# Odd batches of an RWKV-7 layer get work tiles of their own, and projections and early stages alternate

## The chip, the cores and the metric

The kernel runs on one core of one Trainium2 chip. The metric is the device time of one execution in microseconds (us), median of three runs. The engines are TensorE (PE; PEld is its weight load), VectorE (DVE), ScalarE (ACT), GpSimd (POOL) and SyncE (SP), which issues nearly all DMAs. Each engine and each DMA queue works through its own list in order; between engines there are only semaphores.

## The reference

Two layers with 512 tokens and 1024 features, float32. Each layer is a mixer and a SwiGLU feed-forward block (2816 wide), each between two RMS norms and added to x. The mixer of layer 0 is RWKV-7, that of layer 1 a chunked spatial gating unit. The change lies in RWKV-7:

```
xs = x[None] + xx[None] * mix[:, None, None, :]           # six mixes of a token and the one before
r, k, v = einsum('cbtd,cde->cbte', xs[:3], w_rkv)
decay = exp(-exp(-softplus(-(w0 + tanh(xw @ w1) @ w2)) - 0.5))
a = sigmoid(a0 + (xa @ a1) @ a2);  g = sigmoid(xg @ g1) @ g2
kk = k * k_k / max(norm over a head, 1e-12);  k = k * (1 + (a - 1) * k_a)
S_t = S_{t-1} diag(decay_t) + (S_{t-1} (-kk_t)) (kk_t a_t)^T + v_t k_t^T;   y_t = S_t r_t    # per head, 64 x 64
y = group_norm(y) * gn_w + gn_b + sum(r * k * r_k) * v;   out = (y * g) @ w_o
```

## The kernel before

Products are made of three matmuls: each operand is split into a high part `whi` (ACT, a cast, line 131) and a low part `wlo` (DVE, line 132), and `mm3` (lines 156 to 158) adds high x high, high x low and low x high. Weights arrive as `wraw` (SP, line 138) into two buffers that take turns; the high and the low parts have two buffers each.

The recurrence is worked in chunks of 64 tokens. The 16 heads are cut into four batches of four heads (256 features), and a list of steps, PLAN, gives the order in which the code of the steps is written. A scheduler of the framework, which plays the written code against times of its own while it compiles, then sets the order of each engine's list; where it moves steps, only the lists show it. The steps of batch b:

- **P** (`kr_proj`): k and r of the batch, four groups of 24 matmuls named `proj` (features by tokens), each with one weight.
- **E** (`early`): the small products `w` and `a` (two of three matmuls each), tanh on ACT into `tw` and `ta`, a scan `cum` on DVE, exponentials `Pp` and `Pi`, the sum `ssp` of k squared (PE), Ln and Exp on ACT (a table load ahead of each), and the operands `ma`, `r`, `kk`, `kp` of the recurrence, which go to DRAM (`sa`, `sb`). `bps` is a small product for the bonus term.
- **X** (`mixed_split`): the mix for v, split into eight slices `xsp`, on ACT and DVE. **V** (`v_proj`): 96 matmuls `v` of a quarter of v's columns, with two weights; v goes to DRAM as `Vd`.
- **F** (`front`): loads the operands back (`ST`, `MV`, 64 loads of 64 KB in all) and makes the chunk matrices: `lm` and `bkt` on PE, copies to `LA`, `BX` and `MV`.
- **B** (`back`): inverts the triangular matrices. DVE transposes LA to `LX` and runs 15 steps of two small operations on `Dm`; transposes to `Dn` and `Dt`; then chained 32 x 32 products `Qp`, `Np`, `Tp`, `Q2p`, `T2p` with copies to `bdT`, and `mp` and `gh`, which give the final MV.
- **S** (`scan`): eight serial steps `us` and `Yp`. **N** (`finish`): group norm (`mu`, `va`, `nr_..`, `Y`), bonus (`vt`, `ob`) and gate (`yt`, `gate`).

The written order before is

```
P0 E0 P1 P2 E1 P3 E2 E3 X0 F0 B0 F1 V0 V1 V2 V3 B1 S0 F2 S1 F3 N0 B2 N1 B3 S2 N2 S3 N3
```

Tiles share rooms by tag: a tile with a tag waits until the oldest holder of the tag's buffers is free. `tw` and `ta` of every batch share two buffers `f0`, which Dm of F takes too; `cum` and `kp` share two buffers `gain` with MVt of B; the norm's scratch and Dn take two buffers `hn`; bdT has a room to itself and is cleared once, at the start. So two early stages cannot overlap: the second one's tw waits until the first one's ma is stored.

Of the kernel before, what the change touches and what calls it, by code (L numbers as in the profile page):

```python
# [7 lines left out]
F32 = mybir.dt.float32  # L8
# [5 lines left out]
P = 128  # L14
T = 512
# [4 lines left out]
C = 64  # L20
# [9 lines left out]
BANKS = dict(pa=(3, 4, 0, 7), pb=(1, 2, 5, 6), h0=(1, 2, 5, 6), h1=(3, 4, 0, 7), tr=(1, 2, 5, 6))  # L30
SLOTS = 17
E2 = 7
PLAN = "P0 E0 P1 P2 E1 P3 E2 E3 X0 F0 B0 F1 V0 V1 V2 V3 B1 S0 F2 S1 F3 N0 B2 N1 B3 S2 N2 S3 N3".split()
XV = "xxxessss"
XSLOTS = 13
LAG = 2
# [46 lines left out]
class Trunk:  # L83
# [287 lines left out]
    def rwkv(self, x0, nxt):  # L371
        nc, i, tc = self.nc, self.i, self.tc
        v, a, g = nc.vector, nc.scalar, nc.gpsimd
        mm = nc.tensor.matmul
        with ExitStack() as ctx:
            ep = ctx.enter_context
            rp = ep(tc.tile_pool(name="rp", bufs=1))
# [12 lines left out]
            def e2(name, shape=(P, 2, T), dt=F32):  # L390
                return rp.tile(list(shape), dt, name=name, tag="e2", bufs=E2)
# [7 lines left out]
            def gslot(name, shape):  # L399
                return self.gp.tile(shape, F32, name=name, tag="gain", bufs=2)  # L400
# [22 lines left out]
            g.memset(id32, 0.0)  # L423
            for r in range(0, P, 32):
                a.copy(id32[r:r + 32], self.ident[r:r + 32, r:r + 32])
            bdT = rp.tile([P, 16, 2, C], F32, name="bdT")
            g.memset(bdT, 0.0)


            w1 = s4("w1", [P, KT, 2, 64])  # L430
# [6 lines left out]
            for tt in range(TT):  # L437
                hn = e2("hn", (P, D))
# [149 lines left out]
            def small_split(name, src_fn, b):  # L588

                raw = rp.tile([P, 2 * P], F32, name=name, tag="ss_raw", bufs=1)  # L590
                src_fn(raw, slice(b * 2 * P, (b + 1) * 2 * P))
                hi = rp.tile([P, 2 * P], F32R, name=name + "h", tag="ss_hi", bufs=2)
                lo = rp.tile([P, 2 * P], F32R, name=name + "l", tag="ss_lo", bufs=2)
                self.split(hi, lo, raw)
                return hi, lo
# [12 lines left out]
            def early(b, k, r):  # L608

                wh, wl = small_split("wa2", load_wa2, b)  # L610
                pc = rp.tile([P, 2, NC], F32, name="pc", tag="pc", bufs=4)
                pr = lambda q: 2 * b + q
                fcs = lambda q: slice(q * P, (q + 1) * P)

                tw, ta = (self.f0p.tile([P, 2, T], F32, name=n, tag="f0", bufs=2) for n in ("tw", "ta"))
                for q in q2:
                    acc = self.bank("pe", "w")
                    self.mm3(acc, (wh[0:64, fcs(q)], wl[0:64, fcs(q)]), (hid[0:64, 0, :], hid[0:64, 1, :]), True, True)
                    a.activation(tw[:, q, :], acc, AF.Tanh, scale=0.5, bias=halfb[:, 0, pr(q):pr(q) + 1])
                for q in q2:  # L620
                    acc = self.bank("pe", "a")
                    self.mm3(acc, (wh[64:128, fcs(q)], wl[64:128, fcs(q)]), (hid[64:128, 0, :], hid[64:128, 1, :]), True, True)
                    a.activation(ta[:, q, :], acc, AF.Tanh, scale=-0.5, bias=halfb[:, 1, pr(q):pr(q) + 1])
                v.tensor_scalar(flat(tw), flat(tw), 1.0, None, op0=ALU.add)
                cum = gslot("cum", [P, 2, T])
                for q in q2:
                    v.tensor_tensor_scan(cum[:, q], rmask.rearrange("p c t -> p (c t)"), tw[:, q], 0.0, op0=ALU.mult, op1=ALU.add)
                Pp = e2("Pp", (P, 2, NC, C + 1))
                Ppf = Pp.rearrange("p q c t -> p (q c) t")
                g.memset(Ppf[:, :, 0:1], 1.0)  # L630
                a.activation(Ppf[:, :, 1:C + 1], flat(cum).rearrange("p (c t) -> p c t", t=C), AF.Exp, scale=-DECAY)
                Pi = cum
                a.activation(flat(Pi), flat(cum), AF.Exp, scale=DECAY, bias=lnh[:, 0:1])
                v.tensor_copy(pc, Pp[:, :, :, C])

                kp = gslot("kp", [P, 2, T])
                for q in q2:
                    v.tensor_scalar(kp[:, q, :], ta[:, q, :], hka[:, 0, pr(q):pr(q) + 1], hka[:, 1, pr(q):pr(q) + 1],
                                    op0=ALU.mult, op1=ALU.add)
                v.tensor_tensor(flat(kp), flat(kp), flat(k), op=ALU.mult)  # L640

                ri = tw
                for q in q2:
                    a.activation(ri[:, q, :], k[:, q, :], AF.Square, scale=fv("rwkv_k_k", pr(q)))
                    ssp = self.bank("pe", "ssp")
                    mm(ssp, bones, ri[:, q, :], start=True, stop=True)
                    v.tensor_scalar(ri[:, q, :], ssp, 1e-24, None, op0=ALU.max)
                a.activation(flat(ri), flat(ri), AF.Ln)
                a.activation(flat(ri), flat(ri), AF.Exp, scale=-0.5)
                kk = k  # L650
                for q in q2:
                    v.scalar_tensor_tensor(kk[:, q, :], k[:, q, :], nkk[:, pr(q):pr(q) + 1], ri[:, q, :], op0=ALU.mult, op1=ALU.mult)

                sv = lambda t: flat(t).rearrange("p (c t) -> p c t", t=C)
                ma = ri
                v.tensor_tensor(sv(ma), sv(kk), Ppf[:, :, 0:C], op=ALU.mult)
                v.scalar_tensor_tensor(flat(kk), flat(ta), -1.0, flat(kk), op0=ALU.add, op1=ALU.mult)
                v.tensor_tensor(flat(kk), flat(kk), flat(Pi), op=ALU.mult)
                bps = self.bank("pe", "bps")
                for q in q2:  # L660
                    v.scalar_tensor_tensor(ta[:, q, :], r[:, q, :], fv("rwkv_r_k", pr(q)), kp[:, q, :], op0=ALU.mult, op1=ALU.mult)
                    for c in range(NC):
                        tt, par = c // 2, c % 2
                        mm(bps[par * 64:par * 64 + 64, (tt * 2 + q) * 2:(tt * 2 + q) * 2 + 2], ta[:, q, c * C:(c + 1) * C],
                           hsel, start=True, stop=True)
                BN = rp.tile([P, TT, 2, 2], F32, name="bn", tag="bn", bufs=4)
                v.tensor_copy(BN.rearrange("p t q h -> p (t q h)"), bps[:, 0:16])
                v.tensor_tensor(sv(r), sv(r), Ppf[:, :, 1:C + 1], op=ALU.mult)
                v.tensor_tensor(flat(kp), flat(kp), flat(Pi), op=ALU.mult)
                nc.sync.dma_start(out=sa[b][0], in_=ma)  # L670
                nc.sync.dma_start(out=sa[b][1], in_=r)
                for hd in range(2):
                    for n, t in ((hd, kk), (1 - hd, kp)):
                        nc.sync.dma_start(out=sb[b][head[hd], :, :, n, :].rearrange("p q c t -> p (q c) t"), in_=sv(t)[head[hd]])
                return dict(pc=pc, BN=BN)

            def front(b, o):

# [50 lines left out]
            def back(b, o):  # L729

                MV, BX, LA, Dm = (o[n] for n in ("MV", "BX", "LA", "Dm"))
                LX = e2("LX", (P, 2, 528))

                v.transpose(full(LX), LA.rearrange("p q c (x t) -> p t (q c x)", x=2))
                LAu = LA.rearrange("p q c t -> p (q c) t")

                for r in (0, 64):
                    for z, x in ((r, 0), (r + 32, 32)):
                        a.activation(LAu[z:z + 32, :, x + 16:x + 32], LAu[z:z + 32, :, x + 16:x + 32], AF.Copy,
                                     scale=mk2[z:z + 32, 0, x + 16:x + 17])  # L740
                        g.memset(LAu[z:z + 32, :, x:x + 16], 0.0)
                LXd, Dmd = diag(LX), diag(Dm)
                for j in range(15):
                    n = 15 - j
# [201 lines left out]
            xr, kr, ops, Y = None, {}, {}, {}  # L946
            for n in PLAN:
                f, b = n[0], int(n[1])
                if f == "P":
                    if xr is None:  # L950
                        xr = mixed_split(0, "ssssssss")
                        xx.clear()
                    kr[b] = kr_proj(b)
                elif f == "E":
                    ops[b] = early(b, *kr[b])
                elif f == "X":
                    xs = mixed_split(2, XV)
                elif f == "V":
                    v_proj(xs, [b])
                elif f == "F":  # L960
                    front(b, ops[b])
                elif f == "B":
                    back(b, ops[b])
                elif f == "S":
                    if b == 3:
                        GW.append(gate_weights(b))
                        OB.extend(bonus(b, ops[b]))
                    Y[b] = scan(b, ops[b], (lambda y: finish_half(b, ops[b], y, (0, 1))) if b == 3 else None)
                elif b == 3:
                    finish_half(b, ops[b], Y[b], (2, 3))  # L970
                else:
                    finish(b, ops[b], Y[b])
# [166 lines left out]
```

## Time and profile before

| | |
|---|---|
| median of 3 runs | 1397.12 us (1393.59 to 1397.96) |
| profiled execution | 1395.72 us, its span 1394.0 us |
| mean granted TensorE clock | 0.971 of full speed |
| PE / PEld / DVE / ACT / POOL busy | 96% / 78% / 56% / 42% / 11% |
| RWKV layer, with its output projection | from the start to 487.67 us |
| projections P0 to P3 on PE | 48.78 to 156.68 us |
| scans: S0, S1, S2 begin | 263.3, 315.1, 379.5 us |

How the rows read. A row of grouped instructions has line, engine, operation, output <- input, shapes and count, then busy us and mean ns, and after the second bar the idle time of the engine just before them with the instruction that ended it. A row of the timeline has start, duration, engine, line and names; in brackets stands the idle time before it and what ended it; neighbours of one kind are merged, and a float32 matmul shows as two records. A row of windows has start and end, then length, busy time and number of records of PE, the granted TensorE clock, the busy share of the DMA engines and GB/s.

### The profile page before, as it was taken

The page shows a single profiled execution, that of the slowest core. Times are in us where ns is not written, and L with a number is a line of the kernel's source. Part 1 is how long each engine was busy: PE and PEld are TensorE (multiplying, and loading weights), DVE is VectorE, ACT ScalarE, POOL GpSimd, SP SyncE. Part 2 cuts the span into 40 slices and gives each one's busy share as a digit, 9 for nine tenths or more (in the row PEclk, how much of TensorE's full clock was granted, in tenths as well). Part 3 has the DMA queues.
Part 4 walks back from the last instruction along what each step waited for, and adds up shares of the span by engine and source line. Part 5 has one row for each costly group of instructions (what it writes and reads, how often), then busy time and mean ns, then how long its engine had stood idle before and what let it go on. Part 6 is the DMA issues. An engine that isn't in the chain of part 4 may idle for free.

```text
span 1394.0 us, 21544 instructions
## 1 busy us (share of the span) xinstructions
PE 1332.0 (96%) x8512; PEld 1088.7 (78%) x8512; DVE 783.9 (56%) x1373; ACT 579.2 (42%) x1076; POOL 152.6 (11%) x190
## 2 busy tenths in 40 slices
PE   5999979989799899999999999999999999999998
PEld 3677768878687688888888887878888888888886
DVE  7975776579847565544553225575574554453223
ACT  5665765566543453222322224543463332232121
POOL 5000200111000021111110002010121111110000
PEclk8999979989799999999999999999999999999999
DMA  5145375432214233333322332342223333332231
GB/s 150 36 140 148 108 208 166 127 77 69 92 49 158 61 101 112 91 95 102 91 91 91 103 109 76 107 138 89 91 77 93 103 91 93 103 92 91 91 105 61
DMA packets 209956, 142.00 MB, mean 102 GB/s; under 512 B 59536, under 2 KB 185024, under 8 KB 209856
## 3 DMA queue, kind: packets, MB, share of 16 engines
q1 hardware_dynamic: 208560, 135.91, 33.0%
q0 software_dynamic: 1296, 4.72, 1.0%
q8 instruction: 67, 1.10, 0.3%
q14 instruction: 33, 0.27, 0.1%
HBM read 124.35 MB, written 14.16 MB: 99 GB/s over the span
## 4 chain that ended last, share of the span: by engine, by line
PE 62%; DVE 2%; ACT 0%; issue 0%; DVEq 0%
PE gu L157 12%; PE gu L158 12%; PE gu L156 11%; PE acc L157 8%; PE acc L158 8%; PE acc L156 8%; PE u L158 1%; PE u L157 1%; PE u L156 1%; DVE x L273 1%; PE s L1065 1%; PE ptr L218 0%; DVE hT L59 0%; DVE rt L208 0%; DVE ry L209 0%; DVE hn L270 0%
## 5 line engine op out<-in xcount | busy, mean ns | idle before, releaser
L131 ACT CAST whi<-wraw 128x1024 fp32r<-128x1024 f32 x177 | 185.7, 1049 | 481.3 <-PE gu L157 250.5
L132 DVE TENSOR_TENSOR wlo<-wraw,whi 128x1024 fp32r<-128x1024 f32 x177 | 263.1, 1487 | 206.3 <-ACT whi L131 202.3
L156 PE MATMUL gu<-hT,whi 128*128 128x512 f32 (+1 forms) x768 | 288.8, 378 | 1.8 <-ACT hT L57 1.7
L157 PE MATMUL gu<-hT,whi 128*128 128x512 f32 (+1 forms) x768 | 288.5, 377 | 1.1 <-DVE hT L59 1.1
L158 PE MATMUL gu<-hT,wlo 128*128 128x512 f32 (+1 forms) x768 | 289.5, 378 | 0.0
L156 PEld LDWEIGHTS gu<-hT,whi 128*128 128x128 f32 x768 | 145.0, 190 | 31.5 <-ACT hT L57 2.3
L157 PEld LDWEIGHTS gu<-hT,whi 128*128 128x128 f32 x768 | 144.9, 189 | 30.5 <-DVE hT L59 1.5
L158 PEld LDWEIGHTS gu<-hT,wlo 128*128 128x128 f32 x768 | 145.1, 189 | 28.5 <-issue 0.2
L157 PE MATMUL acc<-wlo,act 128*128 128x512 f32 x416 | 164.0, 394 | 0.0
L156 PE MATMUL acc<-whi,act 128*128 128x512 f32 x416 | 163.5, 394 | 0.0
L158 PE MATMUL acc<-whi,act 128*128 128x512 f32 x416 | 160.4, 394 | 0.0
L332 DVE TENSOR_TENSOR sg<-sg,gu 128x512 f32<-128x512 f32 x44 | 30.3, 688 | 142.2 <-PE gu L158 139.2
L333 POOL TENSOR_TENSOR sg<-sg,hn 128x512 f32<-128x512 f32 x44 | 57.0, 1295 | 417.3 <-DVE sg L332 417.3
L156 PEld LDWEIGHTS acc<-whi,act 128*128 128x128 f32 x416 | 78.2, 188 | 18.1
L158 PEld LDWEIGHTS acc<-whi,act 128*128 128x128 f32 x416 | 78.2, 188 | 18.0
L157 PEld LDWEIGHTS acc<-wlo,act 128*128 128x128 f32 x416 | 78.1, 188 | 18.0
L330 DVE TENSOR_TENSOR sg<-gu,hn 128x512 f32<-128x512 f32 x44 | 30.4, 691 | 66.5 <-PE gu L158 66.3
L131 ACT CAST act<-sg 128x512 fp32r<-128x512 f32 x52 | 32.3, 621 | 71.7 <-POOL sg L333 57.5
L156 PE MATMUL proj<-xsp,whi 128*128 128x512 f32 x128 | 51.6, 403 | 0.0
L158 PE MATMUL proj<-xsp,wlo 128*128 128x512 f32 x128 | 51.1, 401 | 0.0
L157 PE MATMUL proj<-xsp,whi 128*128 128x512 f32 x128 | 50.3, 396 | 0.2 <-DVE xsp L132 0.2
L708 PE MATMUL lm<-MV,ST 128*128 128x128 f32 x256 | 40.0, 309 | 7.0 <-ACT BX L726 3.0
(303 smaller groups left out, 2124.0 us busy)
## 6 DMA issues: line engine op xcount, KB each, us to landing
wraw<-in_ffn_w_gate_dram SPq DMA_DIRECT2D x44, 512.0 KB
wraw<-in_ffn_w_up_dram SPq DMA_DIRECT2D x44, 512.0 KB, 3.8
wraw<-in_ffn_w_down_dram SPq DMA_DIRECT2D x44, 512.0 KB, 3.7
wraw<-in_rwkv_w_rkv_dram SPq DMA_DIRECT2D x24, 512.0 KB, 3.7
wraw<-in_sgu_w_in_dram SPq DMA_DIRECT2D x16, 512.0 KB, 3.7
x<-in_x_dram SPq DMA_DIRECT2D x8, 512.0 KB, 3.2
MV<-sa SPq DMA_DIRECT2D x64, 64.0 KB, 2.5
ST<-sb SPq DMA_DIRECT2D x8, 512.0 KB
```

The lines of the kernel that those rows point to most:

```text
L131: self.nc.scalar.copy(hi, src)
L132: self.nc.vector.tensor_tensor(lo, src, hi.bitcast(F32), op=ALU.subtract)
L156: mm(out, lhs[0], rhs[0], start=start, stop=False)
L157: mm(out, lhs[0], rhs[1], start=False, stop=False)
L158: mm(out, lhs[1], rhs[0], start=False, stop=stop)
L273: v.scalar_tensor_tensor(xts[tt][:, c], f, y[:, 0:1], xts[tt][:, c], op0=ALU.mult, op1=ALU.add)
L330: nc.vector.tensor_tensor(sg, pp[0], yb, op=ALU.mult)
L332: nc.vector.tensor_tensor(sg, sg, pp[1], op=ALU.mult)
L333: nc.gpsimd.tensor_tensor(sg, sg, yb, op=ALU.mult)
L708: mm(lm[:, cc * P:(cc + 1) * P], st[:, cc].rearrange("p n t -> p (n t)"), mv[:, :, cc, hd, :], start=True, stop=True)
L1065: mm(acc[:, tt * P:(tt + 1) * P], vt[tt][:, m * P:(m + 1) * P], wsT[:, m, :], start=True, stop=True)
```

## The change

Odd batches (E1, E3) get rooms of their own in the early stage: tw and ta are the two halves of a tile `tws` that lies in the room of bdT (new tag `bd`), and cum and kp lie in the two buffers `hn`. Even batches keep the old rooms. bdT is therefore taken and cleared when B0 begins, not at the start. And PLAN alternates: E1 is written ahead of P2, and E2 ahead of P3.

```diff
-PLAN = "P0 E0 P1 P2 E1 P3 E2 E3 X0 F0 B0 F1 V0 V1 V2 V3 B1 S0 F2 S1 F3 N0 B2 N1 B3 S2 N2 S3 N3".split()
+PLAN = "P0 E0 P1 E1 P2 E2 P3 E3 X0 F0 B0 F1 V0 V1 V2 V3 B1 S0 F2 S1 F3 N0 B2 N1 B3 S2 N2 S3 N3".split()
...
-            bdT = rp.tile([P, 16, 2, C], F32, name="bdT")
-            g.memset(bdT, 0.0)
+            bd = lambda name, shape: rp.tile(shape, F32, name=name, tag="bd", bufs=1)
...
-                tw, ta = (self.f0p.tile([P, 2, T], F32, name=n, tag="f0", bufs=2) for n in ("tw", "ta"))
+                if b % 2:
+                    tws = bd("tws", [P, 2, 2, T])
+                    tw, ta = tws[:, 0], tws[:, 1]
+                    room = lambda name: self.sm.tile([P, 2, T], F32, name=name, tag="hn", bufs=2)
+                else:
+                    tw, ta = (self.f0p.tile([P, 2, T], F32, name=n, tag="f0", bufs=2) for n in ("tw", "ta"))
+                    room = lambda name: gslot(name, [P, 2, T])
...
-                cum = gslot("cum", [P, 2, T])
+                cum = room("cum")
...
-                kp = gslot("kp", [P, 2, T])
+                kp = room("kp")
...
+            inv = []
...
+                if not inv:
+                    inv.append(bd("bdT", [P, 16, 2, C]))
+                    g.memset(inv[0], 0.0)
+                bdT = inv[0]
```

The number and kind of PE, ACT and DVE instructions stay the same; the scheduler's lists differ from P2 on. Three places, each as a list before and one of the change.

SP, the DMA queue, in the V stage. `wraw` of 128x4x256 is a V weight; sa and sb are stores of an early stage, MV, ST and BX loads of F. Before, ahead of the second V1 weight and the first V2 weight (the last row; the three V weights ahead of them came before any load of MV):

```order
L682 DMA ST<-sb 128x2x512
L674 DMA sb<-kp 1024x1x64 x2
L682 DMA ST<-sb 128x2x512
L689 DMA MV<-sa 64x4x64 x15
L702 DMA BX<-ident 64x4x64 x2
L583 DMA Vd<-vev 128x2x256
L670 DMA sa<-tw 128x1024
L583 DMA Vd<-vev 128x2x256
L138 DMA wraw<-in_rwkv_w_rkv_dram 128x4x256 x2
```

E3's store of ma is the row sa<-tw. In the change the last row is the pair of V2 weights (both V0 and both V1 weights came earlier); E3's stores of ma (sa<-tws), kk and r stand further up:

```order
L710 DMA BX<-ident 64x4x64
L680 DMA sb<-kp 1024x1x64 x2
L710 DMA BX<-ident 64x4x64 x7
L697 DMA MV<-sa 64x4x64 x13
L690 DMA ST<-sb 128x2x512 x2
L697 DMA MV<-sa 64x4x64 x3
L710 DMA BX<-ident 64x4x64 x2
L582 DMA Vd<-vev 128x2x256 x2
L138 DMA wraw<-in_rwkv_w_rkv_dram 128x4x256 x2
```

The V1 weights moved ahead of the loads, and V2's behind those of F0 and F1: from sa<-tws to the V2 pair there are 43 issues.

DVE, the end of B1's inverses, where N0's norm runs too. Before (Y less its mean, then the last copy to bdT, then the rest of the norm):

```order
L877 TENSOR_TENSOR Y<-Y,mu 128x1024
L716 TENSOR_TENSOR BX<-BX,mk_128 128x256
L805 COPY bdT<-T2p 32x16x32
L711 TENSOR_TENSOR MV<-lm,mk_128 64x4x2x64
L881 TENSOR_REDUCE va<-hn 128x16
L893 TENSOR_TENSOR hn<-hn,bn 128x4x128 x2
L165 TENSOR_SCALAR nr_a<-va 128x16
```

In the change:

```order
L173 SCALAR_TENSOR_TENSOR nr_t<-nr_t,nr_a 128x16
L174 SCALAR_TENSOR_TENSOR nr_y<-nr_t,nr_y 128x16
L895 TENSOR_TENSOR Y<-Y,nr_y 128x1024
L746 STREAM_TRANSPOSE LX<-LA 128x1024
L724 TENSOR_TENSOR BX<-BX,mk_128 128x256
L759 TENSOR_TENSOR tm<-LX,Dm 128x2x15
L761 TENSOR_TENSOR Dm<-Dm,tm 128x2x15
L817 COPY bdT<-T2p 32x16x32
```

The copy to bdT moved behind the whole norm and behind the transpose LX that begins B2.

DVE, the copies of B2's Tp and Q2p, where N1's norm and an output weight's split run too. Before:

```order
L881 TENSOR_REDUCE va<-hn 128x16
L749 TENSOR_TENSOR Dm<-Dm,tm 128x2x12x4
L893 TENSOR_TENSOR hn<-hn,bn 128x4x128
L165 TENSOR_SCALAR nr_a<-va 128x16
L893 TENSOR_TENSOR hn<-hn,bn 128x4x128
L747 TENSOR_TENSOR tm<-LX,Dm 128x2x55
L132 TENSOR_TENSOR wlo<-wraw,whi 128x1024
L167 TENSOR_SCALAR nr_h<-nr_a 128x16
L786 COPY bdT<-Tp 32x16x32
L749 TENSOR_TENSOR Dm<-Dm,tm 128x2x11x5
L169 TENSOR_SCALAR nr_y<-nr_h 128x16
L796 COPY Q_4024<-Q2p 32x512
```

In the change (LX and Dm belong to B3):

```order
L746 STREAM_TRANSPOSE LX<-LA 128x1024
L798 COPY bdT<-Tp 32x16x32
L724 TENSOR_TENSOR BX<-BX,mk_128 128x256
L887 TENSOR_REDUCE mu<-Y 128x16
L759 TENSOR_TENSOR tm<-LX,Dm 128x2x15
L132 TENSOR_TENSOR wlo<-wraw,whi 128x1024
L888 TENSOR_SCALAR mu<-mu 128x16
L761 TENSOR_TENSOR Dm<-Dm,tm 128x2x15
L889 TENSOR_TENSOR Y<-Y,mu 128x1024
L759 TENSOR_TENSOR tm<-LX,Dm 128x2x28
L808 COPY Q_4022<-Q2p 32x512
L798 COPY bdT<-Tp 32x16x32
```

Both copies of Tp and that of Q2p now stand ahead of va and hn, with one weight split between them.

## Prediction

> **What bounds the kernel now.** I read the page first, then a table of windows cut at stage borders, then the idle rows inside the two worst windows, then the DMA queue (SP) and VectorE (DVE) there. The page:
>
> ```profile
> span 1394.0 us, 21544 instructions
> PE 1332.0 (96%) x8512; PEld 1088.7 (78%) x8512; DVE 783.9 (56%) x1373; ACT 579.2 (42%) x1076; POOL 152.6 (11%) x190
> PE   5999979989799899999999999999999999999998
> ```
>
> TensorE (PE) is the bound: 96% busy, and from the fifteenth of the forty slices (34.85 us each) on it has no hole. What can be won lies in the first 488 us, the RWKV layer. Its stages (start and end; length, PE busy, granted clock, DMA share):
>
> ```profile
> 48.78:156.68 107.90, 107.73 (x493) 1.00 0.43 123
> 156.68:217.69 61.01, 52.05 (x366) 0.83 0.68 179
> 217.69:263.32 45.63, 42.67 (x732) 0.93 0.35 109
> 263.32:315.09 51.77, 46.05 (x797) 0.90 0.44 114
> 315.09:347.53 32.44, 30.83 (x395) 1.00 0.30 73
> 347.53:379.47 31.94, 24.03 (x425) 0.68 0.30 93
> ```
>
> The borders: first projection; first V matmul; first matmul of V's third column group (V2); first scan step of S0; of S1; end of S1's last step; first step of S2. The projections P0 to P3 run dense at full clock, so what E1 waits for today (rooms that E0 still holds) costs PE nothing. The losses are in the second row (9.0 us idle and clock 0.83: 52.05 x 0.17 = 8.8 us more, so 43.2 us of dense work take 61.0) and in the last (7.9 idle, clock 0.68). Who ends the idle time of the second:
>
> ```profile
> L157 PE MATMUL v<-wlo,xsp 128*128 128x256 f32 x64 | 21.1, 330 | 1.0 <-DVE wlo L132 1.0
> L708 PE MATMUL lm<-MV,ST 128*128 128x128 f32 x64 | 11.9, 354 | 5.5 <-ACT BX L726 3.0 <-POOL Dm L696 1.5 <-POOL Dm L695 0.7
> L664 PE MATMUL bps<-hsel,ta 128*64 128x2 f32 x64 | 2.8, 212 | 1.2 <-DVE ta L661 1.2
> L721 PE MATMUL bkt<-ident,ST 128*128 128x128 f32 x16 | 2.7, 291 | 1.0 <-ACT BX L715 1.0
> ```
>
> There E2 and E3 run their long DVE and ScalarE (ACT) chains between F0 and V. The change pulls E2 in front of P3, and gives E1 and E3 rooms of their own, so Dm of F0 no longer waits for E3's stores.
>
> **Term A, the V stage.** Ahead of V stand now E2's two ssp, its bps, and E3's twelve matmuls w and a, by these rows:
>
> ```profile
> 75.53 1.88 PE L646 MATMUL ssp<-tw,bones 128*128 128x512 f32 x4
> 136.31 1.10 PE L664 MATMUL bps<-hsel,ta 128*64 128x2 f32 x32
> 66.29 0.39 PE L158 MATMUL a<-hid,wa2l 64*128 64x512 f32 x1
> 66.53 0.39 PE L156 MATMUL a<-hid,wa2h 64*128 64x512 f32 x1
> 282.30 2.05 PE L708 MATMUL lm<-MV,ST 128*128 128x128 f32 x16
> ```
>
> 1.88 + 1.10 + 12 x 0.24 (start to start) = 5.9 us: V starts at 156.7 + 5.9 = 162.6. No wait is added in the projections: each weight is split one group of 24 matmuls ahead, and the first stage row has no idle time to lose. The order of the changed kernel puts two more units of F1's lm (2 x 2.05), four bkt and eight mvt (0.6 and 1.2 by the groups above) ahead of V2, 5.9 us that came after it before; that is as much as left. So dense work alone ends at 162.6 + 43.2 = 205.8 instead of 217.7. Two waits stand against it.
>
> First, X0's last two splits are written behind E3's k step (L652) on DVE, which waits for Ln and Exp on ACT:
>
> ```profile
> L652 DVE SCALAR_TENSOR_TENSOR k<-k,nkk,tw 128x512 f32<-128x512 f32 x4 | 2.8, 750 | 2.9 <-ACT tw L649 2.9
> 173.40 0.28 PE L664 MATMUL bps<-hsel,ta 128*64 128x2 f32 x4 [1.25 <-DVE ta L661]
> 176.00:180.00 4.00, 4.00 (x31) 0.50 0.83 214
> ```
>
> Bounds 0 (V gets there later) and 2.9 (it waits the step out); I take 2.7, since V reaches its seventh slice while that step runs. The other two rows show what a wait costs behind itself: after 1.25 us idle the clock is at 0.50. Six us at half clock are 3 us, added to each wait; 211.5. The Trainium skill ("TensorE: Matmul & The Clock Gate", Part 1) has the clock fall only after an idle window of about 3.4 us; by that these 3 us, and the next 3, would drop out and the sum would be 6 us better. The trace disagrees (1.25 us were enough), so I keep them.
>
> Second, V2's weights. SP issues in order:
>
> ```profile
> 184.55 1.88 PE L646 MATMUL ssp<-tw,bones 128*128 128x512 f32 x4
> 183.82 9.88 SPq L689 DMA_DIRECT2D MV<-sa  x15
> 196.95 0.33 SPq L670 DMA_DIRECT2D sa<-tw  x1
> 197.81 1.64 SPq L138 DMA_DIRECT2D wraw<-in_rwkv_w_rkv_dram  x2
> 205.69 2.34 DVE L132 TENSOR_TENSOR wlo<-wraw,whi 128x1024 fp32r<-128x1024 f32 x2
> ```
>
> One issue takes 9.88 / 15 = 0.66 us, and before, two V weights were stuck at 197.81 behind E3's store of ma. In the new order the V1 weights go ahead of F0's loads, but V2's come 43 issues behind E3's store. That store follows E3's ssp by 10.5 us (186.43 to 196.95): the ssp ends ten V matmuls and 1.88 us into V, about 165.7, so the store goes at 176 to 178; 43 x 0.66 = 28 us more, with a wait for E3's kp about 209. From issue to the first split's end took about 9 us at 197.81 (205.69 + 1.17); with DVE free perhaps 6.5: V2 starts at about 216 and not 211.5, and a second cold start costs 3. Bounds: 205.8 (weights in time) and 221 (9 us, and that split stands deep in the Dm loop). At 216 PE is 1.7 us early with 5.9 us more done, less 3: **A = -4.6 us**.
>
> The memset of bdT moves from the start into B0: 1.81 us on POOL, which is 11% busy, some 20 us ahead of the copy that needs it; without that cover it would cost its 1.8.
>
> ```profile
> 3.27 1.81 POOL L427 MEMSET bdT<- 128x2048 f32 x1
> ```
>
> **Term B, start of S1.** Before, B1's last bdT copy came ahead of most of N0's group norm on DVE; now the whole norm and the transpose LX of B2 stand ahead of it, and mp of B1 waits for that copy.
>
> ```profile
> 294.22 0.99 PE L778 MATMUL Np<-Qs,Dt 32*32 32x32 f32 x40
> 301.85 1.22 DVE L875 TENSOR_REDUCE mu<-Y 128x16 f32<-128x1024 f32 x1
> 307.55 0.69 DVE L805 COPY bdT<-T2p 32x512 f32<-32x512 f32 x1 [0.17 <-ACT bdT L805]
> 308.30 1.16 PE L810 MATMUL mp<-MVt,bdT 128*128 128x128 f32 x8
> 311.74 1.29 DVE L893 TENSOR_TENSOR hn<-hn,bn 128x512 f32<-128x512 f32 x2 [1.52 <-DMA hn<-Vd]
> 314.57 1.95 DVE L734 STREAM_TRANSPOSE LX<-LA 128x1024 f32<-128x1024 f32 x1
> ```
>
> S0 now ends ahead of Np, so mu can start near 293, not 301.85. From there: five large steps (four of 1.2, LX 1.95) 6.8; hn with its wait 2.8; four copies of 0.69, 2.8; eleven small ones at about 0.17, 1.9; two MV 1.4; ACT's square and copy 1.5: 17.2, with a later Vd load about 312. mp comes 3.7 late. Bounds 0 (B1 late anyway) and 8: **B = +4**, nearest to the count.
>
> **Term C, the gap between S1 and S2.** PE starves there for B2:
>
> ```profile
> 356.48 0.71 PE L781 MATMUL Tp<-Dt,Qs 32*32 32x32 f32 x36
> 359.87 0.69 DVE L893 TENSOR_TENSOR hn<-hn,bn 128x512 f32<-128x512 f32 x1 [1.67 <-DMA hn<-Vd]
> 361.34 1.22 DVE L132 TENSOR_TENSOR wlo<-wraw,whi 128x1024 fp32r<-128x1024 f32 x1
> 362.55 0.67 DVE L786 COPY bdT<-Tp 32x512 f32<-32x512 f32 x1
> 366.00 1.91 PE L801 MATMUL T2p<-bdT,Q 32*32 32x32 f32 x64 [0.29 <-ACT bdT L786]
> 379.47 0.33 PE L846 MATMUL us<-su,MV 128*64 128x64 f32 x2
> ```
>
> Tp ended at 357.2, its copies to bdT came at 362.55 behind hn (which waits for a load) and a weight split, and T2p at 366. In the new order these copies come ahead of va and hn, with Tp spread into S1's steps. T2p could run near 358, 8 us earlier; two splits of 1.22 still stand ahead of the last bdT copy, and N1's vt and yt ahead of S2 on PE. Bounds 0 and 10: **C = -5.3**. S3 and the rest are PE work in nearly the old order; I let them follow.
>
> **Sum:** -4.6 + 4 - 5.3 = -5.9 against the profiled execution's 1395.7: 1389.8. The median of the runs shown is 1.4 above that execution: **1391 us**.
>
> **Rivals.**
> 1. The V stage loses less, because both waits fall away: for it speaks that E2's chain is out of the stage and that the V1 weights now come early; against it the row of 15 issues. PE then reaches V2 at 205.8 instead of 216, 10 us and 3 of clock; B0's Dm loop on DVE, which cannot start before F0's last lm, takes about 5 back: 1383. On this the Trainium skill ("DMA: Bandwidth & Descriptors", Issuing engines are not separate DMA queues) says that a sequencer's time to start a DMA is usually small beside the DMA. The trace has 0.66 us for each of fifteen in a row. The clock rule cited above would give 1385 in the same place.
> 2. No change: A is won and B keeps it, with C at 0 because B2's mp still waits for N1's hn load: -4.6 + 4 + 0, with half a us of PE order either way: 1396 to 1398.
> 3. Slower: N0 on DVE becomes the bound of S1. If its Vd load lands 8 us later than I have it (it stands behind four loads of F3's MV on SP, which wait for S0's rooms), the last bdT copy, mp and S1 slip 12 us; F3 takes S1's rooms, so S2 and S3 slip too and C is lost: -4.6 + 12 = +7.4, 1404. It decides from a slip of about 9 us on. Against it: that load's wait was 1.52 before.
>
> **Chances.** What this kernel's timing can tell is about 0.3%, 4.2 us: faster is below 1392.9, slower above 1401.3. Forecast 0.45 (its own range 1386 to 1396, two thirds of it faster), rival 1 0.17, rival 2 0.20, rival 3 0.18. Faster 0.30 + 0.17 = 0.47; same 0.15 and 0.18 of rival 2, 0.33; slower the rest, 0.20. Range: half of rival 1, the forecast, rival 2 and the near part of rival 3: 1382 to 1402.
>
> **What the profile after would show.** A: V's first matmul near 162.6; idle of PE at a v matmul released by a DVE split near 173; the second pair of V weights issued near 209 and V2 starting near 216. B: LX ahead of the last bdT copy, mp of B1 near 312, S1 near 318. C: T2p of B2 within 10 us of S1's last step, the window from S1's end to S2 under 27 us, its clock above 0.68. I am wrong if V2 starts before 210 or after 221, if S1 starts before 312 or after 323, or if the gap before S2 stays at 32.

## The result and the profile after

The change makes the kernel slower: 1405.0 us against 1397.04 (medians of 11 runs each on the same chip; one run of before read 4482 us and is left out of the interval), ratio 1.0059, 95% interval 1.0042 to 1.0077, so 8 us. The forecast was 1391 and the range ended at 1402. The profiled execution took 1407.42 us, 2.4 above that median. Its page, in the rows shown of before:

```profile
span 1405.7 us, 21558 instructions
PE 1337.6 (95%) x8512; PEld 1092.1 (78%) x8512; DVE 785.2 (56%) x1373; ACT 577.2 (41%) x1076; POOL 152.7 (11%) x190
PE   5999988989789989999999999999999999999998
```

In the row of the forty slices (35.1 us each) little shows: the sixth, in the V stage, rose from 7 to 8, the seventh and the twelfth fell from 9 to 8 (and the fourteenth and the fifteenth changed places). The windows tell more; they are cut at the same events as before (but the first keeps before's 48.78, while the projections began here at 47.80, and the second ends where V2 runs on), and from S2 on three more (S2 to B3's first T2p; to the end of S3's steps; to the feed-forward block):

```profile
48.78:163.12 114.34, 113.39 (x538) 1.00 0.48 134
163.12:221.32 58.20, 47.82 (x363) 0.88 0.63 169
221.32:265.62 44.30, 42.52 (x718) 0.89 0.30 89
265.62:324.58 58.96, 50.20 (x789) 0.83 0.37 101
324.58:356.20 31.62, 31.06 (x540) 1.00 0.31 76
356.20:381.34 25.14, 17.72 (x240) 0.73 0.32 95
381.34:414.07 32.73, 29.70 (x589) 0.90 0.22 68
414.07:454.56 40.49, 38.13 (x375) 0.96 0.37 116
454.56:498.44 43.88, 38.91 (x174) 0.92 0.23 73
```

The same three stages of before:

```profile
379.47:405.72 26.25, 24.41 (x542) 1.00 0.19 59
405.72:441.95 36.23, 36.02 (x399) 1.00 0.40 126
441.95:487.67 45.72, 39.54 (x180) 0.96 0.24 76
```

S0's stage (fourth row) grew from 51.77 to 58.96 us and fell in clock from 0.90 to 0.83. The gap behind S1 (sixth) shrank from 31.94 to 25.14, as forecast. The three stages behind it grew by 6.5, 4.3 and -1.8. The feed-forward block starts 10.8 us later and takes 907.3 us instead of 906.3.

Since work moves between stages, lengths alone mislead. The next table has the time that PE lost in each stage, its length less busy time x clock, summed over the rows of a stage; "before held" and "after held" are the two kernels `rooms0` and `ctl` below, which run the lists of before and of after once more and show how far one profile can be trusted (FFN is the feed-forward block):

```
stage            before  before held  after  after held   mean, after less before
P0 to first V      0.2       0.5       1.0      0.9              +0.6
V to S0           24.2      22.5      23.0     20.3              -1.7
S0 to S1          10.3      10.0      17.3     18.9              +7.9
S1 and the gap    17.3      17.5      12.8     14.3              -3.8
S2 to FFN          9.6      11.6      18.6     14.8              +6.1
S0 starts        263.3     262.1     265.6    264.7              +2.5
S1 starts        315.1     313.6     324.6    324.6             +10.2
FFN starts       487.7     487.1     498.4    496.5             +10.1
```

All of the loss is there when S1 starts. Behind it the gain in the gap is taken back before the feed-forward block. A loss of PE's time names the stage in which it shows, not yet its cause.

### The profile page after: what moved, and what is told of

Same layout as the page of the kernel before. It is cut to its first block, busy times and chain, and to the rows that moved or that the text cites. A ratio compares the mean times of both kernels' runs of the same rounds, so it can differ in the third digit from the quotient of the medians.

```text
span 1405.7 us, 21558 instructions
## 1 busy us (share of the span) xinstructions
PE 1337.6 (95%) x8512; PEld 1092.1 (78%) x8512; DVE 785.2 (56%) x1373; ACT 577.2 (41%) x1076; POOL 152.7 (11%) x190
## 4 chain that ended last, share of the span: by engine, by line
PE 84%; DVE 7%; ACT 3%; DMA 3%; issue 2%; SPq 1%; POOL 0%; DVEq 0%; ACTq 0%; POOLq 0%
PE gu L158 11%; PE gu L156 11%; PE gu L157 11%; PE acc L156 9%; PE acc L157 9%; PE acc L158 9%; PE proj L158 2%; PE proj L156 2%; PE proj L157 2%; PE lm L716 2%; PE lora L506 1%; PE gh L829 1%; PE u L158 1%; PE u L156 1%; PE u L157 1%
## 5 line engine op out<-in xcount | busy, mean ns | idle before, releaser
L158 PEld LDWEIGHTS acc<-whi,act 128*128 128x128 f32 x416 | 78.2, 188 | 18.1
L157 PEld LDWEIGHTS acc<-wlo,act 128*128 128x128 f32 x416 | 78.1, 188 | 18.1
L156 PE MATMUL proj<-xsp,whi 128*128 128x512 f32 x128 | 51.8, 405 | 0.0
```

The lines of the kernel that those rows point to most:

```text
L156: mm(out, lhs[0], rhs[0], start=start, stop=False)
L157: mm(out, lhs[0], rhs[1], start=False, stop=False)
L158: mm(out, lhs[1], rhs[0], start=False, stop=stop)
```

## Experiments

After an ordinary edit the scheduler makes other lists, so that far more moves than was meant. So the experiments hold the lists: each kernel carries the order of every engine's list as a table, and ties each instruction to the one before it by an order alone, without a semaphore.

```diff
+    for e, text in LISTS.items():
+        own = [x for x in code if str(x.engine) == "EngineType." + engines[e]]
+        ...
+        row = [own[n] for n in np.cumsum(steps.astype(np.int64))]
+        for p, q in zip(row, row[1:]):
+            tc.add_manual_dep(q, p.name, how, reason="list")
```

Rooms and lists can so be taken apart, and single instructions moved. All ratios are to the kernel before on the same chip; kernels that ran on different chips are compared by these ratios.

### Rooms or lists, and from which stage on

`rooms0`: the rooms of the change (tws in `bd`, cum and kp in `hn`, bdT cleared in B0), all lists as before.

> The changed kernel's rooms and the written order of before, with every engine's list held exactly as in before (the one instruction left free is the clearing of bdT). It splits the change into its rooms and its lists. If the loss of 8 us comes from the lists alone: 1397 us, within 2 us of before. If the rooms themselves cost (a tile waits for its new holder, or bdT is cleared late): above 1400 us, with a new wait between 100 and 230 us.

Measured 1395.06 us, ratio 0.9998 (0.9983 to 1.0012). The rooms together with holding the lists cost less than 2 us by this interval; the loss comes with the lists. `ctl`, the lists of after held in the same way, is the partner of the later experiments:

> The changed kernel with every engine's list held exactly as it is: the comparison for the three runs beside it, since single executions of these kernels differ by up to 8 us. 1403 to 1407 us; a difference from the changed kernel's 1405 would be an effect of holding the lists.

Measured 1406.42, 1.0065 (1.0044 to 1.0087): like the change itself.

`ha_S0`, `ha_S1`, `ha_S2`: the lists of after up to the first step of S0, S1 or S2, and from there those of before. `hb_S1`: the lists of before up to S1, then those of after. Where two lists are joined there is a seam: what one has already done and the other not yet lands there.

> The changed kernel with its own lists up to the first step of S0 (265.6 us in its trace) and, from there, the lists of before on every engine, for what is then left. Theory 1 (the loss is made in three places, by lost TensorE time of each stage, after against before: +0.8 in the projections, -1.7 in the V stage, +0.5 up to S0, +7.0 in S0's stage, -1.0 in S1, -3.4 in the gap, +4.2 and +3.7 in S2 and S3): only -0.4 of it is kept here, so 1396 to 1399 us. Rival (the early lists set the later stages back whatever order follows): 1402 to 1406 us.

> The changed kernel's lists up to the first step of S1 (324.6 us), before's lists from there. Theory 1: S0's stage, with the copy to bdT behind N0's norm, costs 7.0 us; this run is 6 to 7 us above the run cut at S0, 1402 to 1405 us. Rival (what S0's stage loses is slack, since S1's gap to S2 waits for B2 anyway): within 2 us of the run cut at S0.

> The changed kernel's lists up to the first step of S2 (381.3 us), before's lists from there. Theory 1: the shorter gap gives 4.4 us back against the run cut at S1, so 1398 to 1401 us, and the lists of S2 and S3 are what costs the rest up to 1405. Rival (the gap was shortened only by leaving 6 us of TensorE work undone before S2, and S2 and S3 lose time because that work is still there): 1404 to 1406 us, no better than the changed kernel.

> The rooms of the change; the lists of before up to the first step of S1 (315.1 us in its trace), the changed kernel's lists from there. It is term C alone: B2's copies early on VectorE, the gap before S2 short. If the prediction's C holds: 1391 to 1393 us, faster than before by 4 to 5. Theory now, from the runs cut at S1 and of the whole change, which take the same time (1405): C gives nothing, since TensorE starts S2 earlier with as much less work done; 1395 to 1398 us, no difference from before.

```
kernel   median us  ratio (95%)               S0     S1     S2     FFN starts
ha_S0    1400.04    1.0030 (1.0015, 1.0045)   265.0  320.2  383.4  495.8
ha_S1    1404.95    1.0057 (1.0035, 1.0079)   265.2  324.9  384.3  496.1
ha_S2    1412.69    1.0108 (1.0089, 1.0128)   263.3  325.7  392.3  505.3
hb_S1    1412.43    1.0130 (1.0112, 1.0148)   260.4  324.5  382.9  497.9
```

With the new lists up to S1 alone the time is that of the whole change; up to S0 alone about half of the loss is there, which neither expectation had. From S1 to the feed-forward block ha_S1 took 171.2 us with the old lists and ctl 171.9 with the new: behind S1 the two are worth the same. The other two kernels are misses, since their seams cost more than what they were to show: in ha_S2 the left-over work of the gap stands ahead of S2, and in hb_S1 N0's vt, yt and gate and F3's lm stand ahead of S1, which starts 19.6 us behind B1's first mp instead of 6.8. They say nothing on the part of the gap. How much of ha_S0 and ha_S1 is their seam isn't known either: ha_S0 took 55.2 us from S0 to S1, with the old lists there, where before took 51.8.

### The V stage

In the changed kernel V1's matmuls end at 196.6, and V2 starts at 218.8. In order: PE's groups from there to V2; the queue SP (between its first row and the next stand 20 loads of F1); ACT and PE at the end of the stretch; and DVE:

```profile
L716 PE MATMUL lm<-MV,ST 128*128 128x128 f32 x48 | 9.1, 356 | 4.5 <-DMA ST<-sb 1.9 <-issue 1.6 <-ACT BX L723 1.0
L772 PE MATMUL mvt<-ident,MV 128*128 128x128 f32 x16 | 3.6, 388 | 2.7 <-ACT MVt L775 1.2 <-ACT BX L723 0.8 <-ACT BX L734 0.8
```

```profile
190.19 6.17 SPq L710 DMA_DIRECT2D BX<-ident  x7
...
209.90 1.08 SPq L582 DMA_DIRECT2D Vd<-vev  x2
211.28 1.25 SPq L138 DMA_DIRECT2D wraw<-in_rwkv_w_rkv_dram  x2
```

```profile
215.23 0.59 ACT L581 COPY vev<-v 128x512 f32<-128x512 f32 x1
217.01 0.58 ACT L581 COPY vev<-v 128x512 f32<-128x512 f32 x1
217.61 1.05 ACT L131 CAST whi<-wraw 128x1024 fp32r<-128x1024 f32 x1
```

```profile
218.83 0.78 PE L156 MATMUL v<-whi,xsp 128*128 128x256 f32 x2
221.32 0.58 PE L157 MATMUL v<-wlo,xsp 128*128 128x256 f32 x1 [1.72 <-DVE wlo L132]
```

```profile
211.77 0.69 DVE L719 TENSOR_TENSOR MV<-lm,mk 64x512 f32<-64x512 f32 x1 [4.27 <-PE lm L716]
```

V2's weights were issued at 211.28, 2.3 us later than forecast (209). V0's stores to Vd (L582) stood in the same row of issues, at 209.90. The room that V1's results are copied to (`vev`, two buffers) comes free with them, so V1, done at 196.6, left its banks only at 215.2 and 217.0, and the cast of V2's first weight stands right behind the second of these copies. Until then PE had F1's products alone, with waits (7.2 us in the two groups), and the last row shows DVE, in the middle of B0's Dm loop, waiting 4.27 us for one of them.

`v2fill` mends this in the new lists: on SP V0's stores and V2's weights go ahead of seven BX loads and F1's loads, on PE V2's matmuls fill the stretch, and two of F1's groups of products go behind B0's Qp; the copies and splits on ACT and DVE follow. Stores and weights move together, so it doesn't tell the one from the other.

```
 SP:  sb<-kp x2
+     Vd<-vev x2            (issued at 189.41)
+     wraw<-in_rwkv_w_rkv x2    (at 192.27)
      BX<-ident x7
      MV<-sa x13 ... ST<-sb x2 ... MV<-sa x3
      BX<-ident x2
-     Vd<-vev x2
-     wraw<-in_rwkv_w_rkv x2
```

> The changed kernel's lists with the V stage's end put in another order: on SP the stores of V0 and the loads of the V2 weights go ahead of seven BX and all F1 loads (before, 30 and 27 issues later); the casts, splits and evacuations of V1 to V3 follow on ScalarE and VectorE; on TensorE 64 matmuls of V2 fill the stretch from 198 to 215 us, in which F0's last unit and mvt wait; F1's first two units move behind Qp of B0 and Q2p, so that B0's 15 steps run without their copies between. Term A: if the store of V0 and the V2 weights, stuck on SP, are what the V stage lost, Qp of B0 comes near 219 to 222 (228.65), S0 near 257 to 260 (265.62), and the kernel takes 1397 to 1400 us. Rival (the stretch is bound by F1's operands and rooms, so what V2 fills is missing later): S0 within 2 us of 265.6 and 1403 to 1407 us.

Measured: B0's first Qp at 219.33 (226.41 in ctl, 228.65 in the change), S0 at 260.2 (264.7 in ctl), S1 319.3, S2 376.6, S3 416.4, FFN 493.5 (496.5). The median is 1404.31, ratio 1.0057 (1.0043 to 1.0072) beside ctl's 1.0065: about 1 us, which these intervals don't tell from nothing. S0 comes where the theory had it and the time where its rival had it: the stage can be shortened by 4.5 us in this way, but that gives back little of the loss.

### The start of S1

B1's last steps and N0 on DVE, in the changed kernel, and when PE waited for them:

```profile
298.04 1.22 DVE L887 TENSOR_REDUCE mu<-Y 128x16 f32<-128x1024 f32 x1 [1.01 <-ACT Y L873]
...
306.53 1.29 DVE L905 TENSOR_TENSOR hn<-hn,bn 128x512 f32<-128x512 f32 x2 [2.32 <-DMA hn<-Vd]
307.94 0.69 DVE L798 COPY bdT<-Tp 32x512 f32<-32x512 f32 x1
...
313.51 1.95 DVE L746 STREAM_TRANSPOSE LX<-LA 128x1024 f32<-128x1024 f32 x1
...
316.15 0.69 DVE L817 COPY bdT<-T2p 32x512 f32<-32x512 f32 x1
```

```profile
309.29 2.02 PE L813 MATMUL T2p<-bdT,Q 32*32 32x32 f32 x64 [0.90 <-ACT bdT L798]
...
316.89 1.16 PE L822 MATMUL mp<-MVt,bdT 128*128 128x128 f32 x8 [0.78 <-DVE bdT L817]
```

N0 starts with mu (first row). Not one copy of B1 but three stand behind parts of it: the second of Tp waits out the Vd load of hn (2.32 us), and T2p with it, 12.7 us behind Np instead of 10.8. From T2p to mp it is 7.6 us instead of 3.3, since the last copy waits for the norm and for LX ahead of it on DVE.

`b_before` tests the last copy by itself, in the lists of before, by moving one DVE instruction behind N0's hn products:

```diff
-L817 COPY bdT<-T2p
 L719 TENSOR_TENSOR MV<-lm,mk
 L893 TENSOR_REDUCE va<-hn
 L905 TENSOR_TENSOR hn<-hn,bn x2
 L165 TENSOR_SCALAR nr_a<-va
+L817 COPY bdT<-T2p
```

> The lists of before, held, with one instruction moved: on VectorE the last bdT copy of B1 goes behind N0's two hn products and nr_a (from 307.5 to about 313 us), which is term B by itself. If the chain from B1's mp over S1 and F3's loads to B3 and S3 sets the end: mp, S1 and S3 5 to 6 us later and the time 4 to 6 us above before, 1401 to 1403. Rival (B3 has slack: its transposes end 16.6 us ahead of its Qp in the trace of before): S1 later by as much, S3 and the time within 2 us of before.

Measured 1402.52, ratio 1.0038 (1.0023 to 1.0052), 5 us slower. The copy and PE's wait for it, first in rooms0, then in b_before:

```profile
306.09 0.69 DVE L817 COPY bdT<-T2p 32x512 f32<-32x512 f32 x1 [0.17 <-ACT bdT L817]
306.83 1.16 PE L822 MATMUL mp<-MVt,bdT 128*128 128x128 f32 x8
```

```profile
311.42 0.69 DVE L817 COPY bdT<-T2p 32x512 f32<-32x512 f32 x1
312.25 2.05 PE L822 MATMUL mp<-MVt,bdT 128*128 128x128 f32 x8 [5.72 <-DVE bdT L817]
```

A copy 5.3 us later makes mp 5.4 later, S1 7.4 later (321.06 against 313.62, though S0 had begun 1.3 earlier) and the program about 5, as expected. In the lists of before, what delays that copy delays the end.

The other direction, in the lists of after: `bcopy` moves B1's copies (bdT, Q) ahead of N0's norm on DVE, and the ACT partner of the last one; `fixAB` is bcopy and v2fill together.

```diff
 L165 TENSOR_SCALAR nr_a<-va
-L798 COPY bdT<-Tp
+L798 COPY bdT<-Tp x2
+L808 COPY Q<-Q2p
 L167 TENSOR_SCALAR nr_h<-nr_a
 ...
+L817 COPY bdT<-T2p
 ...
 L761 TENSOR_TENSOR Dm<-Dm,tm
-L817 COPY bdT<-T2p
```

> The changed kernel's lists with four copies to bdT and Q2 moved, and nothing else: on VectorE the second Tp copy, the Q2 copy and the last bdT copy of B1 go ahead of the rest of N0's norm and of B2's transpose, on ScalarE the other last bdT copy goes ahead of two LA copies. Term B: if the order of these copies costs what the prediction said, mp of B1 comes 4 us earlier (near 313 instead of 316.89), S1 near 320.5, and the kernel takes 1400 to 1402 us. Rival (S1 starts late because B1 as a whole is late, and N0's norm must be done then or soon after): S1 within 1.5 us of 324.6 and 1404 to 1406 us.

> Both edits of the two runs before this one. If A and B are separate and each as large as thought: the sum of the two gains against the changed kernel, 1392 to 1397 us, as fast as before or faster. If they overlap (the same wait counted twice): no better than the better of the two.

Measured 1406.28 (1.0082, 1.0059 to 1.0105) and 1405.10 (1.0071, 1.0047 to 1.0096): nothing gained beside ctl's 1.0065. In bcopy T2p came 3 us earlier and the copy 2.5 us behind it, but:

```profile
306.30 1.20 PE L813 MATMUL T2p<-bdT,Q 32*32 32x32 f32 x64
...
312.24 2.05 PE L716 MATMUL lm<-MV,ST 128*128 128x128 f32 x8 [2.75 <-ACT BX L723]
...
314.94 1.91 PE L822 MATMUL mp<-MVt,bdT 128*128 128x128 f32 x8
```

On PE lm and vt still stand ahead of mp, and lm waits for ACT's copies. S1 started at 324.69 (324.57 in ctl).

`s1fix` therefore puts the end of B1 (copies, mp, gh, and the first steps of S1) ahead of most of N0 and of half of F3's lm, on all engines; `v2s1` is s1fix and v2fill.

> The changed kernel's lists with B1's end put ahead of N0 on all engines: the bdT and Q2 copies as in the run before, and now also, on TensorE, mp and gh of B1 and the first steps of S1 ahead of N0's transposes vt and yt, its gate products and half of F3's lm; VectorE's additions to MV, ScalarE's copies of mp and the store of N0 on SP follow. Theory 2: mp comes near 312 (316.9), S1 near 318 (324.6), the second unit of F3's loads, which waits for B1's additions, near 318 (324.7), LX of B3 some 5 us earlier than 356.7, and the time is 4 to 7 us under the control run. Rival (N0 has to be done at that place in any case, for its rooms, and only changes places with S1): S3 within 2 us of the changed kernel's and the time as the control run's.

> The V stage's end reordered (V2 early) and B1's end ahead of N0, both on the changed kernel's lists. If theory 2 holds and the V stage's gain of 3 to 5 us at S0's start goes through the same chain: 8 to 11 us under the control run, 1394 to 1397 us, as fast as before. If the V stage's gain is lost in S0's stage as in the earlier run: as the run with B1's end alone.

Measured 1413.90 (1.0122, 1.0092 to 1.0153) and 1412.57 (1.0113, 1.0090 to 1.0136), both worse than either expectation. The copy came in time, mp at 313.2, S1 at 321.6, but S1 then ran for 43.8 us instead of 31.4:

```profile
321.56:365.36 43.80, 41.18 (x554) 0.81 0.22 54
```

What was put off now stands between S1's serial steps.

The last try was in the lists of before. `t2_first` puts B1's T2p on PE between the halves of one lm group, and its copies, mp and gh earlier on all engines:

```diff
-L716 MATMUL lm<-MV,ST x8
+L716 MATMUL lm<-MV,ST x4
 L813 MATMUL T2p<-bdT,Q
+L716 MATMUL lm<-MV,ST x4
+L822 MATMUL mp<-MVt,bdT x4
```

> The lists of before, held, with B1's end moved up: T2p goes between the two halves of the lm group that stands ahead of it on TensorE (305.0 to about 303.3 us), its two copies to bdT, the first mp, gh and the additions to MV follow. If B1's chain alone sets S1, F3's rooms and S3: mp 2 to 3 us earlier, S1 and S3 2 to 3 us earlier, 1393 to 1394 us, 0.15 to 0.25% under before. Rival (another chain, N0's products and F3's lm on TensorE ahead of S1, ends at the same time): mp earlier, S1 and the time within 1 us of before.

Measured 1399.45, 1.0027 (1.0011 to 1.0043). T2p came 40.0 us behind S0's first step instead of 41.7, and mp 43.7 instead of 45.0, but S1 53.2 instead of 51.8: N0's and F3's products on PE end no earlier. That is the rival, and the time is worse than the rival had it; in this execution T2p also took 1.92 us, 1.20 in rooms0, so part of it can be the clock. No version beat the kernel before.

### The gap behind S1

`slowc` undoes the third place in the lists of after: B2's copies of Tp and Q2p go behind N1's hn products again.

```diff
-L798 COPY bdT<-Tp
 ...
 L759 TENSOR_TENSOR tm<-LX,Dm
-L808 COPY Q<-Q2p
-L798 COPY bdT<-Tp
 ...
 L905 TENSOR_TENSOR hn<-hn,bn x2
+L798 COPY bdT<-Tp
+L808 COPY Q<-Q2p
+L798 COPY bdT<-Tp
```

> The changed kernel's lists with C undone by itself: on VectorE the two Tp copies and the Q2 copy of B2 go behind N1's two hn products, as they stood before, and on ScalarE their partners follow. T2p of B2 comes 4 to 6 us later and with it S2 (381.3 in the changed kernel's trace). Theory 2 (the end is set by the chain gh of B1, rooms of F3, F3's loads and lm, B3, S3, on which B2 and S2 do not lie): S3 and the time stay within 2 us of the control run. Rival (the prediction's sum: what S2 loses, the kernel loses): 4 to 6 us above the control run.

Measured 1411.06, 1.0098 (1.0074 to 1.0121), 4.6 us above ctl on the same chip, as its rival had it; the two intervals just overlap. B2's T2p, in ctl and in slowc:

```profile
368.05 1.92 PE L813 MATMUL T2p<-bdT,Q 32*32 32x32 f32 x64 [0.70 <-ACT bdT L798]
```

```profile
376.24 1.92 PE L813 MATMUL T2p<-bdT,Q 32*32 32x32 f32 x64 [0.43 <-ACT bdT L798]
```

S2 moved from 381.5 to 389.5, 7.9 us, of which S1 was 2.9 late already. So in the new lists that place is worth about 5, near its forecast 5.3.

`c_before` does it alone in the lists of before: the copies ahead of hn, and on PE B2's T2p ahead of N1's vt and mp ahead of its second vt and of yt.

```diff
+L798 COPY bdT<-Tp
+L808 COPY Q<-Q2p
+L798 COPY bdT<-Tp
 L905 TENSOR_TENSOR hn<-hn,bn
 L165 TENSOR_SCALAR nr_a<-va
 ...
-L798 COPY bdT<-Tp
-L808 COPY Q<-Q2p
-L798 COPY bdT<-Tp
```

> The lists of before, held, with C alone: B2's Tp and Q2 copies on VectorE ahead of N1's hn products and of a weight's split, their partners on ScalarE and the last bdT copies moved up as well, T2p and the first mp on TensorE ahead of N1's vt. If C is a gain of its own: T2p near 361.5 (366.0), mp near 366 (370.4), S2 2 to 5 us earlier, and 1391 to 1395 us, faster than before. Rival (what B2 wins, N1 loses, and S2 waits for N1's yt and gate on TensorE): S2 within 1.5 us of 379.5 and 1395 to 1399 us.

Measured 1401.35, 1.0031 (1.0013 to 1.0048), slower than either expectation. PE:

```profile
359.87 1.92 PE L813 MATMUL T2p<-bdT,Q 32*32 32x32 f32 x64 [2.78 <-ACT bdT L798]
364.33 1.30 PE L822 MATMUL mp<-MVt,bdT 128*128 128x128 f32 x8
367.95 0.63 PE L933 MATMUL yt<-ident,Y 128*128 128x128 f32 x4 [1.88 <-ACT ob L910]
...
376.83 0.66 PE L933 MATMUL yt<-ident,Y 128*128 128x128 f32 x4 [1.54 <-DVE ob L938]
377.42 0.33 PE L858 MATMUL us<-su,MV 128*64 128x64 f32 x2
```

T2p and mp ran 4.1 us earlier than in rooms0 (359.9 and 364.3 against 364.0 and 368.4), but S2 started at 377.4 all the same (377.5): N1's yt and gate stand ahead of it on PE, and N1 is what had been put off. S3's start slipped from 414.5 to 417.7. So the place is a gain only where N1 is already further, and N1 is further in the new lists because N0 ran earlier, at the cost of S1's start. I take the two for one trade; that is argued from these runs and not shown, since no kernel had the one without the other.

## Why the prediction was wrong, point by point

**V's start: right, in part by luck.** 163.1 against 162.6; the projections with the new work in them took 7.4 us longer and not 5.9, but began 1.0 earlier (47.80). The wait for X0's split was 0.53 us instead of 2.7, with no cold stretch behind it, which should have made the stage 5 us better than forecast.

**Term A (-4.6): failed, in two steps.** By S0 1.1 us less had been lost in all, with the projections. The first step that failed is the start of V2, 216: its first matmuls came at 218.8, it ran on from 221.3, and PE starved before. The weights were issued 2.3 us late, and from there to the end of their first split it was 10.0 us (211.28 to 221.27), not 6.5. I had read the row of 43 issues only for the weights: V0's stores were stuck in it too, and with them V1's copies, which stand ahead of the cast on ACT. What the stores and what the weights cost is not told apart. The second step is the credit: I took 5.9 us of F1's work done early as won. By S0 3.5 us more had been done than before and 2.5 us more time had passed. And ha_S0, with that work done and the old lists from there, took 55.2 us from S0 to S1 and not less than rooms0's 51.5, so nothing shows that the work done early shortened that stage.

**Term B (+4): the mechanism was right, the size was not.** mp came at 316.9 (312 forecast) and S1 at 324.6 (318), past the 323 at which I had said I would be wrong. The count of what stands on DVE from mu to the last copy was good, 17.2 us counted and 18.1 measured (298.04 to 316.15). The step that failed is mu's start: 298.04 and not near 293. I had S0 end ahead of Np, which ran at 294.22 before; S0's last step ended at 296.7, and Np itself came at 296.60. That two copies of Tp wait behind N0's Vd load as well (+1.9 to T2p) I had not priced, but T2p was done before the last copy's turn came. By PE's lost time the stage lost 7.9 us more, just inside the range for B, 0 to 8; mp itself came 8.6 us later than before.

These 7.9 us are not all B's. In ha_S0, with the old lists there, PE loses some 18 us of that stage too (55.20 less 47.24 x 0.78), as in ctl (59.89 less 49.42 x 0.83), and the stage is 3.4 us longer than before's 51.8. The rest of the lengthening, 3.8 us to the change and 4.7 to ctl, comes with the new lists of the stage, as does the step from ha_S0's ratio to ha_S1's, 0.27%. Whether the first part is F1's work done early, which left PE idle here, or ha_S0's seam, is open.

**Term C (-5.3): right in the new lists.** The gap is 25.1 (under 27), undoing it costs 4.6, and S1 with the gap lost 3.8 us less by the table. Of the other signs, its clock was 0.73 here (over 0.68) but 0.60 in ctl, and T2p came 11.8 us behind S1's end and not within 10, a miss. The 5.3 itself was a choice between the bounds: the working has 8 us less two splits of 1.22, 5.6.

**"S3 and the rest, I let them follow" (0): failed, +6.1.** F3's second group of MV loads waits for rooms that B1's additions to MV free: in both traces the first of them is issued within 0.03 us of the end of such an addition. SP, after and before:

```profile
302.96 0.60 SPq L901 DMA_DIRECT2D hn<-Vd  x1
324.74 0.58 SPq L697 DMA_DIRECT2D MV<-sa  x1
```

```profile
316.85 2.56 SPq L689 DMA_DIRECT2D MV<-sa  x4
```

So a late end of B1 is a late F3. B3's LX, after and before:

```profile
356.75 1.98 DVE L746 STREAM_TRANSPOSE LX<-LA 128x1024 f32<-128x1024 f32 x1 [1.40 <-ACT LA L722]
```

```profile
348.47 1.96 DVE L734 STREAM_TRANSPOSE LX<-LA 128x1024 f32<-128x1024 f32 x1
```

Its Dm loop ended 12 us later (386.4 against 374.4) and S3 started 7.5 later. But B3's Qp began 6.2 us behind the last transpose even so (12.7 before), so it isn't held by the loop itself; on PE it stands behind N1's yt, which waited 1.33 us (at 391.42) for an `ob` that DVE did behind the two transposes. So the term is mis-sized, the late loads are seen, and what carries the rest of the 6.1 is open: no kernel tried this chain by itself, and 4 us of it come and go between two executions of the same lists (18.6 and 14.8 in the table; see the last section).

**The rivals.** The time came out at rival 3's 1404, and its place was right, N0 on DVE ahead of B1's last copy. Its mechanism was not: the Vd load of N0 was issued at 302.96, earlier than before, and hn waited 2.32 us for it instead of 1.52. N0 as a whole stands ahead, not its load. And C was not lost but paid back later. So the time was right there by luck. The sum by the stages of my terms, as measured: -1.1 + 7.9 - 3.8 + 6.1 = 9.1, beside 10.1 at the start of the feed-forward block and 8 in the medians.

## What to carry to other kernels

When a change lets one chain run ahead on an in-order engine, price every instruction of the delayed chain that now stands behind it, and then follow the rooms that the delayed chain frees: here one late tail held up a later step's loads by 8 us. When weights or loads wait in a queue, list all that waits with them, stores above all, since a store frees the room that another engine needs to empty a bank. Work that an engine does early is a gain only if it would have stood on the path later; take nothing for it until the row that it shortens is found.

## What the runs showed of the hardware that I had not expected

PE's clock halved after a stall of 1.67 us (1.44 in ctl) that no semaphore explains, in the middle of small 32 x 32 products. In the changed kernel:

```profile
405.38 0.48 PE L793 MATMUL Tp<-Dt,Qs 32*32 32x32 f32 x19 [1.67 <-issue]
409.97 0.63 PE L158 MATMUL acc<-whi,oT 128*128 128x512 f32 x1
410.39 0.63 PE L156 MATMUL acc<-whi,oT 128*128 128x512 f32 x1
412.67 0.39 PE L157 MATMUL acc<-wlo,oT 128*128 128x512 f32 x1
412.90 0.40 PE L158 MATMUL acc<-whi,oT 128*128 128x512 f32 x1
```

The granted clock is 0.50 from 405.4 to 411; from 409.5 to 411.7 the matmuls go 0.42 us apart, later 0.23.

Lists alike, and the clock not: in the same stretch ahead of the feed-forward block after ran at 0.70 and ctl at 1.00, so that this stretch alone differs by some 2.5 us between two executions of the same lists.

```profile
481.00:491.00 10.00, 9.77 (x33) 0.70 0.07 29
```

```profile
481.00:491.00 10.00, 9.22 (x46) 1.00 0.13 47
```

Both executions wait there for the same cast, 2.11 us (to 481.24 and to 481.78), so the length of a wait alone doesn't settle whether the clock falls; what does isn't shown.

Single executions of one kernel mostly lay within 4 us on either side of its median, and this is one place where that arises. That is why stage tables here stand on two profiles for each set of lists.
